# Token-half sums of a feed-forward layer kept in PSUM, with the norm ahead of the weights' sums

## The chip, the cores and the metric

The kernel runs on one core of a Trainium2 chip. The metric is the device time of one execution in microseconds (us). One core has a TensorE for matmuls (PE), with its weight loads shown apart (PEld), a VectorE (DVE), a ScalarE (ACT), a GpSimd (POOL), a SyncE whose queue starts the transfers (SP), and eight PSUM banks into which matmuls write.

## The reference, cut to what matters

A block of two layers works on 512 latent tokens and 256 context tokens, 1024 wide. The mixer of a layer is not touched. What is touched is the start of the feed-forward part:

```
def swiglu(h, w1, w3, w2):
    return (jax.nn.silu(h @ w1) * (h @ w3)) @ w2

x = x + ga_f * swiglu(rmsnorm(x, g_ffn[i]) * (1.0 + sc_f) + sh_f, w1[i], w3[i], w2[i])
ctx = ctx + cga_f * swiglu(rmsnorm(ctx, g_ffn[i]) * (1.0 + csc_f) + csh_f, w1[i], w3[i], w2[i])  # layer 0 only
```

`rmsnorm` divides each token by the root of its mean square. The inner width is 2816.

## The kernel before, in words

**The product in seven.** `h @ w1` and `h @ w3` are cut into jobs; a job is one of the two matrices, a part q and a chunk i. A job is computed as a 2x2 block product by a Winograd scheme of seven products in place of eight. Tokens are cut in two halves (layer 0: 384 and 384 columns, layer 1: 256 and 256), the 1024 inputs in two halves of four chunks of 128. b11 is the first half of the inputs for the first token half, b12 for the second, b21 and b22 the second half of the inputs. Product 1 needs b11 and product 2 needs b21. Products 7, 4, 5, 3 and 6 need sums, differences or copies of the four blocks: these are the operands, tiles `hp`, each held as a high and a low half (`hi` cast on ACT, `lo` the rest, on DVE or POOL). The weights of a product are sums of four blocks of the matrix in the same way (`wr` in, `S` and `wr` the sums, `wp` the two halves). Each product is 4 chunks by 3 matmuls (high by high, low by high, high by low; lines 398 to 400), 12 in all, into one PSUM bank (`f`). The program has eight of these banks and hands each bank out again when its last reader is done.

**The start of a layer's feed-forward.** `first_products` runs product 1 and then product 2 of the four lead jobs side by side. Then `run` goes on with the first two jobs alone, product by product, in the order 6, 7, 4, 5, 3 (`STEPS` without its first two), each for job 0 and then for job 1; the third job follows. While products 1 and 2 run, two chains of other work go on:

- `first_norm` makes the operands of products 1 and 2 from the first token half.
- `prepare` makes the rest. It is a generator: `first_products` takes a number of its steps after each chunk of products 1 and 2 (`PREP`), `run` one at every second product. It first takes the norm of the second token half: `rstd` is the reciprocal root, brought to all partitions by a matmul into a PSUM bank (line 619) after a reciprocal on DVE (line 615). `scaled` multiplies x by gain and `rstd` on DVE (line 1471, tile `hn`), `shifted` adds the bias on ACT (line 1479, tile `hf`). Four rounds then form, for each chunk, b12 - b11, T2 = b22 - that (operand of 6) and b21 - T2 (lines 1515, 1517, 1523 to 1525). Line 1528 makes the operand of 7, and `put` (lines 1461 and 1462) the two halves of the operands of 7, 4, 5 and 3 in that order.

**The weights.** `WeightStream.pump` runs ahead of the products. When the next task is one of a job's products it forms the sums that this product needs (`form`, lines 225 to 229, on DVE), casts the high half on ACT (line 183) and takes the low half on POOL or, for some products of `w1`, on DVE (line 188). It goes on until the weight tiles are used up, so the sums of the first two jobs stand in DVE's queue as soon as the tiles allow, whatever else waits behind them.

**What sets the order.** Every engine takes its instructions in the order in which the program was written out. An operation waits for the data and also for the last reader of the tile or PSUM bank that it overwrites.

**Results.** `complete` adds each product into the sums U (u[2], u[3]); `block` forms the gate (lines 1630, 1631) or the gated product (1634, 1635). Product 1's bank is copied out by ACT (line 1592).

Of the kernel before, what the change touches and what calls it, by code (L numbers as in the profile page):

```python
# [41 lines left out]
PREP = (0, 1, 1, 2), (1, 1, 1, 2)  # L42
# [4 lines left out]
STEPS = (1, 2, 6, 7, 4, 5, 3)  # L47
NCOL = 0.4219
# [10 lines left out]
class Job:  # L59
# [7 lines left out]
    def __init__(self, key, steps, time, pos=None):  # L67
        self.key, self.steps, self.time, self.pos = key, steps, time, pos
        self.units, self.raw, self.used, self.formed = None, {}, set(), set()
        self.u, self.home = {}, {}  # L70

# [30 lines left out]
class WeightStream:  # L102
# [6 lines left out]
    def __init__(self, kern, raws, parts):  # L109
# [7 lines left out]

        self.lead, self.dve = {}, {}
# [6 lines left out]

    def add_step(self, job, p, aps):
# [4 lines left out]
        if 1 in self.USES[p] and job.units[1] is None:  # L131
# [19 lines left out]
    def there(self, task):  # L151
# [4 lines left out]
        return all(i in what.raw or what.units[i] in self.raw for i in self.USES[p])  # L156
# [54 lines left out]
    def form(self, job, p):  # L211
# [5 lines left out]
        for i in self.USES[p]:  # L217
# [10 lines left out]
        if p == 7:  # L228
            v.tensor_sub(a12, a12, a11)  # L229
# [1134 lines left out]
class FeedForward:  # L1364
# [10 lines left out]
    def plan(self):  # L1375
# [59 lines left out]
    def begin(self, x, acc, streams, out):  # L1435
# [3 lines left out]
        self.h = [None] * NK  # L1439
        self.t = {}  # L1440
        self.prep = self.prepare()
        self.norm1 = Norm(self.first_norm())
# [21 lines left out]
    def scaled(self, rs, st, i):  # L1464

        k = self.k
        if self.h[i] is None:
            self.h[i] = k.act(name="hf")
        t = k.tmp(name="hn")
        for s, sl, at in pieces(st):  # L1470
            k.nc.vector.scalar_tensor_tensor(
                t[:, at], self.x[i][:, sl], k.gs[:, self.layer, 1, s, i : i + 1], rs[:, at], op0=OP.mult, op1=OP.mult
            )
        return t

    def shifted(self, t, st, i):
        k = self.k
        for s, sl, at in pieces(st):
            k.nc.scalar.activation(self.h[i][:, sl], t[:, at], AF.Identity, bias=k.mod[:, self.layer, 3, s, i : i + 1])

    def first_norm(self):
        st, n = self.streams[0], self.n
        nc = self.k.nc
        rs = yield from self.k.rstd(self.acc[st], st[1])
        yield 0
        for i in range(NK + 1):
            j = i - 1
            if i < NK:
                t = self.scaled(rs, st, i)
            if i > 0:  # L1490
                hi, lo = self.operand(1 + j // 4, j % 4)
                nc.scalar.copy(hi, self.h[j][:, :n])
            if i < NK:
                self.shifted(t, st, i)
            if i > 0:
                (nc.gpsimd if j % 2 else nc.vector).tensor_sub(lo, self.h[j][:, :n], hi.bitcast(F32))
                yield 0

    def prepare(self):

        st, n = self.streams[1], self.n
        nc = self.k.nc
        v = nc.vector
        rs = yield from self.k.rstd(self.acc[st], st[1], False)
        yield 0

        def block(e, i):
            return self.h[i + 4 * (e // 2)][:, n * (e % 2) : n * (e % 2) + n]
# [739 lines left out]
```

## Time and profile before

| | |
|---|---|
| three runs | 1699.99, 1701.46 and 1704.0 us, median 1701.46 |
| profiled execution | 1700.14 us, of which the span from the first to the last instruction is 1698.4 |
| mean granted clock of TensorE | 0.982 |
| busy: PE, PEld | 1601.1 us (94%), 1449.0 us (85%) |
| busy: DVE, POOL, ACT | 1178.8 us (69%), 818.6 us (48%), 741.9 us (44%) |

In the trace a row of an engine has its start, its duration, the line, the operation, the tile written and those read, and in brackets how long the engine stood idle ahead of it and which instruction ended that. Layer 0's feed-forward begins with product 1 at 448.0 us, layer 1's at 1307.6 us.

### The profile page before, as it was taken

How to read it: one execution, taken by the hardware profiler on the slowest of the kernel's cores; microseconds unless marked ns; L12 is line 12 of the kernel's file. 1: busy time of each engine (PE TensorE's matmuls, PEld its weight loads, DVE VectorE, ACT ScalarE, POOL GpSimd, SP SyncE). 2: the span in 40 equal slices, each digit the busy share in tenths (PEclk: the TensorE clock that was granted, in tenths of full speed). 3: DMA queues.
4: the chain of work that ended last, by engine and by line, in shares of the span. 5: the costliest groups of instructions: out<-in, count | busy, mean ns of one | idle time of the engine just before them, and what ended most of it. 6: DMA issues, size and time to landing. Idle time of an engine off the chain costs nothing. (4 is left out here: it accounts for less than half of the span.)

```text
span 1698.4 us, 26272 instructions
## 1 busy us (share of the span) xinstructions
PE 1601.1 (94%) x9730; PEld 1449.0 (85%) x9730; DVE 1178.8 (69%) x2054; ACT 741.9 (44%) x1437; POOL 818.6 (48%) x601
## 2 busy tenths in 40 slices
PE   6989999999979998999999999999999799999996
PEld 4867788888979987899999997779789789999996
DVE  6866566773777899586766776665666876766685
ACT  5534444653553223242332554444554544344343
POOL 3443232123375556465555623444125676666672
PEclk9999999999989999999999999999999899999998
DMA  9364253353023343434443345422232132332322
GB/s 355 139 199 138 67 160 97 119 170 130 26 76 111 103 134 120 129 125 137 149 137 118 127 161 163 135 73 74 80 131 81 60 115 75 111 114 76 94 87 69
DMA packets 76384, 202.28 MB, mean 119 GB/s; under 512 B 12704, under 2 KB 19488, under 8 KB 75872
## 3 DMA queue, kind: packets, MB, share of 16 engines
q1 hardware_dynamic: 76256, 200.60, 36.5%
q8 instruction: 77, 1.26, 0.3%
q14 instruction: 51, 0.42, 0.1%
HBM read 184.25 MB, written 11.80 MB: 115 GB/s over the span
## 5 line engine op out<-in xcount | busy, mean ns | idle before, releaser
L188 POOL TENSOR_TENSOR wp<-wr,wp 128x512 fp32r<-128x512 f32 (+1 forms) x336 | 465.7, 1399 | 311.0 <-ACT wp L183 306.2
L398 PE MATMUL f<-hp,wp 128*128 128x384 f32 (+1 forms) x1232 | 386.8, 314 | 14.8 <-DVE U L1599 4.2
L399 PE MATMUL f<-hp,wp 128*128 128x384 f32 (+1 forms) x1232 | 387.1, 314 | 10.8 <-DVE wp L188 6.2
L400 PE MATMUL f<-hp,wp 128*128 128x384 f32 (+1 forms) x1232 | 385.2, 313 | 4.0 <-POOL hp L1524 4.0
L183 ACT CAST wp<-wr 128x512 fp32r<-128x512 f32 (+1 forms) x360 | 213.3, 609 | 309.4 <-PE f L400 118.5
L188 POOL TENSOR_TENSOR wl<-wr,wh 128x1024 fp32r<-128x1024 f32 (+2 forms) x75 | 163.8, 2188 | 346.4 <-ACT wh L183 266.4
L398 PEld LDWEIGHTS f<-hp,wp 128*128 128x128 f32 x1232 | 238.0, 193 | 18.8 <-issue 8.2
L399 PEld LDWEIGHTS f<-hp,wp 128*128 128x128 f32 x1232 | 238.4, 193 | 15.3 <-POOL wp L188 8.5
L400 PEld LDWEIGHTS f<-hp,wp 128*128 128x128 f32 x1232 | 238.1, 193 | 5.1 <-POOL hp L1524 5.1
L398 PE MATMUL proj<-h,wh 128*128 128x512 f32 (+1 forms) x456 | 165.0, 362 | 1.0 <-DVE v L404 1.0
L398 PE MATMUL f<-g,wp 128*128 128x512 f32 (+1 forms) x468 | 160.5, 343 | 5.4 <-ACT g L1461 5.4
L400 PE MATMUL f<-g,wp 128*128 128x512 f32 (+1 forms) x468 | 160.5, 343 | 0.0
L399 PE MATMUL f<-g,wp 128*128 128x512 f32 (+1 forms) x468 | 160.3, 342 | 0.0
L399 PE MATMUL proj<-h,wl 128*128 128x512 f32 (+1 forms) x456 | 159.1, 349 | 0.7 <-POOL wl L188 0.7
L400 PE MATMUL proj<-h,wh 128*128 128x512 f32 (+1 forms) x456 | 158.9, 348 | 0.0
L1658 DVE SCALAR_TENSOR_TENSOR x<-f,mod,x 128x512 f32<-128x512 f32 (+1 forms) x130 | 79.0, 622 | 69.5 <-PE f L400 69.3
L398 PEld LDWEIGHTS proj<-h,wh 128*128 128x128 f32 x456 | 86.6, 190 | 25.5 <-issue 6.6
L522 DVE CUSTOM_DVE_ANT_0 adj<-wr,tab 128x1024 bf16<-128x1024 f32 x64 | 104.6, 1653 | 4.1 <-DMA wr<-in_w_adat_dram 4.0
L398 PEld LDWEIGHTS f<-g,wp 128*128 128x128 f32 x468 | 89.1, 190 | 17.0 <-ACT g L1461 6.8
L400 PEld LDWEIGHTS f<-g,wp 128*128 128x128 f32 x468 | 88.9, 190 | 11.2 <-DVE g L1462 1.1
L399 PEld LDWEIGHTS f<-g,wp 128*128 128x128 f32 x468 | 89.1, 190 | 9.9
L399 PEld LDWEIGHTS proj<-h,wl 128*128 128x128 f32 x456 | 86.8, 190 | 11.8 <-POOL wl L188 1.1
(251 smaller groups left out, 3415.2 us busy)
## 6 DMA issues: line engine op xcount, KB each, us to landing
wr<-in_w_dram SPq DMA_DIRECT2D x88, 512.0 KB
wr<-in_w_adat_dram SPq DMA_DIRECT2D x48, 512.0 KB
wr<-in_w_dram SPq DMA_DIRECT2D x80, 256.0 KB
wr<-in_w_ada_dram SPq DMA_DIRECT2D x32, 512.0 KB
ada<-in_w_ada_dram SPq DMA_DIRECT2D x16, 512.0 KB
wr<-in_w_out_dram SPq DMA_DIRECT2D x16, 512.0 KB
tab<-in_rpb_dram SPq DMA_DIRECT2D x12, 512.0 KB
strip<-strips SPq DMA_DIRECT2D x3, 1152.0 KB
```

The lines of the kernel that those rows point to most:

```text
L183: nc.scalar.copy(hi, src)
L188: (nc.vector if vector else nc.gpsimd).tensor_sub(lo, src, hi.bitcast(F32))
L398: mm(out, a[0], b[0], start=start, stop=False)
L399: mm(out, a[1], b[0], start=False, stop=False)
L400: mm(out, a[0], b[1], start=False, stop=stop)
L522: self.nc.vector.tensor_tensor_reduce(out=self.tmp(mybir.dt.bfloat16, D, "adj"), in0=raw, in1=self.tabs[("silu", s)], scale=1.0, scalar=0. ...
L1658: k.nc.vector.scalar_tensor_tensor(xs, ps[:, :n], k.mod[:, self.layer, 5, s, m : m + 1], xs, op0=OP.mult, op1=OP.add)
```

## The change

1. **The order of products** of the first two jobs goes from 6, 7, 4, 5, 3 to 3, 7, 6, 4, 5 (`FIRST`). Product 3 of these jobs needs the weights that were product 6's to form sums with (`uses`), u[2] and u[3] are both kept from product 1 (a second copy on ACT), and `complete` and `block` follow suit.
2. **The weights' sums wait** (`held`): `pump` stops ahead of the first job's product 3 until products 1 are written out, so that the norm of the second half comes ahead of them on DVE.
3. **`prepare` is written anew.** First it makes b22 for all four chunks and from it product 3's operand. Then, chunk by chunk, ACT writes b12 to a PSUM bank (a tile `T`, gain and bias in one step), DVE puts t3 = b22 - b12 in a second bank, and t1 = b12 - b11, the operand of 7 (from t3), t3 + b11 in b12's bank, the operand of 6 (from that) and b21 less it follow. Last come the operands of 5 and 4, chunk by chunk.

The number of matmuls and their shapes stay. DVE gets 12 instructions more (2044 to 2056 in the whole program), ACT 4 more, POOL 16 fewer.

```diff
-PREP = (0, 1, 1, 2), (1, 1, 1, 2)
+PREP = (0, 1, 1, 1), (1, 1, 1, 2)
+FIRST = (3, 7, 6, 4, 5)
...
+    def uses(self, job, p):
+        return (0, 1) if p == job.first else self.USES[p]
...
+        if 0 not in job.raw:
+            return
-        if p == 6:
+        if p == job.first:
             job.s1 = self.k.tmp(name="S1")[:, :n]
             v.tensor_add(job.s1, a21, a22)
             v.tensor_sub(a21, a11, a21)
             v.tensor_sub(a11, job.s1, a11)
-        if p == 7:
+        if p == (3 if job.first == 3 else 7):
             v.tensor_sub(a12, a12, a11)
...
     def pump(self):
             task = self.tasks[self.n_split]
+            if self.held and task[1] is self.held and task[0][1] == self.held.first:
+                self.issue()
+                break
...
-            j.steps = ()
-        self.order = [(j, p) for p in (1, 2) for j in lead] + [(j, p) for p in STEPS[2:] for j in two]
+            j.steps, j.first = (), FIRST[0]
+        self.order = [(j, p) for p in (1, 2) for j in lead] + [(j, p) for p in FIRST for j in two]
...
     def prepare(self):
-        for i in range(5):
-            if i < 4:
-                ts = [(j, self.scaled(rs, st, j)) for j in (i, i + 4)]
-            if i > 0:
-                b11, b12, b21, b22 = (block(e, i - 1) for e in range(4))
-                v.tensor_sub(b11, b12, b11)
-                t2 = self.k.tmp(name="T2")[:, :n]
-                v.tensor_sub(t2, b22, b11)
-            if i < 4:
-                for j, t in ts:
-                    self.shifted(t, st, j)
-            if i > 0:
-                hi, lo = self.operand(6, i - 1)
-                nc.scalar.copy(hi, t2)
-                nc.gpsimd.tensor_sub(lo, t2, hi.bitcast(F32))
-                nc.gpsimd.tensor_sub(b21, b21, t2)
-            yield 0
-        for i in range(4):
-            v.tensor_sub(block(1, i), block(3, i), block(1, i))
-        for p, e in ((7, 1), (4, 2), (5, 0), (3, 3)):
-            for i in range(4):
-                self.put(self.operand(p, i), block(e, i), i % 2)
+        for i in range(5):
+            if i < 4:
+                t = scaled(i + 4)
+            if i > 0:
+                hi, lo = self.operand(3, i - 1)
+                nc.scalar.copy(hi, late[i - 1][0])
+                gp.tensor_sub(lo, late[i - 1][0], hi.bitcast(F32))
...
+        ts = {0: scaled(0)}
+        for i in range(4):
+            b11, b21, (b22, t1) = self.h[i][:, :n], self.h[i][:, n : 2 * n], late[i]
+            b12, t3 = k.ps("T")[:, :n], k.ps("T")[:, :n]
+            shifted(b12, ts.pop(i), i)
+            v.tensor_sub(t3, b22, b12)
+            v.tensor_sub(t1, b12, b11)
+            (hi7, lo7), (hi6, lo6) = self.operand(7, i), self.operand(6, i)
+            nc.scalar.copy(hi7, t3)
+            v.tensor_sub(lo7, t3, hi7.bitcast(F32))
+            v.tensor_add(b12, t3, b11)
+            nc.scalar.copy(hi6, b12)
+            if i < 3:
+                ts[i + 1] = scaled(i + 1)
+            v.tensor_sub(lo6, b12, hi6.bitcast(F32))
+            v.tensor_sub(b21, b21, b12)
+            yield 0
+        for i in range(4):
+            self.put(self.operand(5, i), late[i][1], i % 2)
+            self.put(self.operand(4, i), self.h[i][:, n : 2 * n], 1 - i % 2)
+            if i % 2:
+                yield 0
...
     def first_products(self):
+            k.w.held = None
```

How the instructions stand before and now is shown at three places of layer 0; layer 1 has the same pattern. A number behind a name tells one tile from another. First DVE, from the end of the first token half's squares on, where product 1's last chunk runs. Before (`S` and `wr` are the weights' sums, `rs` the second half's reciprocal, `hn` what is scaled with it):

```order
L597 TENSOR_TENSOR sq_3901<-sq_3901,sq_4367 128x384 [waits DVE_49]
L225 TENSOR_TENSOR S_765_4422<-wr_4268 128x512 [waits DMAHW6_49]
L226 TENSOR_TENSOR wr_4268<-wr_3958,wr_4268 128x512 [waits DMAHW5_49,DVE_49,Pool_49]
L227 TENSOR_TENSOR wr_3958<-S_765_4422,wr_3958 128x512 [waits DVE_49,Pool_49]
L225 TENSOR_TENSOR S_767_4429<-wr_4320 128x512 [waits DMAHW7_49]
L226 TENSOR_TENSOR wr_4320<-wr_4027,wr_4320 128x512 [waits DMAHW2_49,DVE_49]
L227 TENSOR_TENSOR wr_4027<-S_767_4429,wr_4027 128x512 [waits DVE_49,Pool_49]
L615 RECIPROCAL rs_4463<-rs_4463 128x3 [waits Activation_49]
L1471 SCALAR_TENSOR_TENSOR hn_4488<-x_3876,gs,rstd_4251 128x384
```

The same place with the change:

```order
L611 TENSOR_TENSOR sq_3901<-sq_3901,sq_4366 128x384 [waits DVE_49]
L629 RECIPROCAL rs_4449<-rs_4449 128x3 [waits Activation_49]
L1495 SCALAR_TENSOR_TENSOR hn_4473<-x_3876,gs,rstd_4251 128x384
L1504 TENSOR_TENSOR hp_4475<-hf_4308,hp_4475 128x384 [waits Activation_49]
L1520 TENSOR_TENSOR hn_4494<-x_3870,rstd_4448 128x384 [waits PE_49]
L1520 TENSOR_TENSOR hn_4499<-x_3872,rstd_4448 128x384
L1520 TENSOR_TENSOR hn_4507<-x_3874,rstd_4448 128x384 [waits DVE_49]
L236 TENSOR_TENSOR S_786_4527<-wr_4268 128x512 [waits DMAHW6_49]
L237 TENSOR_TENSOR wr_4268<-wr_3958,wr_4268 128x512 [waits DMAHW5_49,DVE_49,Pool_49]
L238 TENSOR_TENSOR wr_3958<-S_786_4527,wr_3958 128x512 [waits DVE_49,Pool_49]
L240 TENSOR_TENSOR wr_3958<-wr_3958 128x512 [waits DVE_49,Pool_49]
```

The reciprocal and the first three `hn` of the second half have moved ahead of the weights' sums, and the sums now stand between the third `hn` and the fourth, eight in a row for the two jobs (line 236 opens each four).

The second place is DVE further on, where the last two chunks' sums are made. Before:

```order
L1515 TENSOR_TENSOR hf_4308<-hf_4308 128x384
L1517 TENSOR_TENSOR T_800_4600<-hf_4407,hf_4308 128x384 [waits DVE_49,Activation_49]
L1515 TENSOR_TENSOR hf_4350<-hf_4350 128x384 [waits Activation_49]
L1517 TENSOR_TENSOR T_802_4623<-hf_4487,hf_4350 128x384 [waits DVE_49,Activation_49,Pool_49]
L1528 TENSOR_TENSOR hf_4297<-hf_4357,hf_4297 128x384
```

The third chunk's turn and the start of the fourth with the change (`T` are the tiles in PSUM, `rstd_4448` the second half's reciprocal root, in PSUM too):

```order
L1553 TENSOR_TENSOR T_4643<-hf_4512,T_4642 128x384 [waits DVE_49,Activation_49]
L1554 TENSOR_TENSOR hf_4512<-T_4642,hf_4308 128x384
L1557 TENSOR_TENSOR hp_4648<-T_4643,hp_4648 128x384 [waits Activation_49]
L1558 TENSOR_TENSOR T_4642<-T_4643,hf_4308 128x384 [waits DVE_49]
L1520 TENSOR_TENSOR hn_4654<-x_3868,rstd_4448 128x384
L1562 TENSOR_TENSOR hp_4649<-T_4642,hp_4649 128x384 [waits Activation_49]
L1563 TENSOR_TENSOR hf_4308<-hf_4308,T_4642 128x384
L1553 TENSOR_TENSOR T_4659<-hf_4566,T_4658 128x384 [waits DVE_49,Activation_49]
```

A chunk's turn has seven DVE operations now, six of which read or write a `T` tile, and the last reader of `rstd_4448` (`hn_4654`) stands in the third chunk's turn, 30 DVE instructions behind the third `hn` of the place above.

The third place is PE, where products 2 end and the first two jobs go on alone. Before, with product 6 of job 0:

```order
L400 MATMUL f_4551<-hp_4494,wp_4419 128x384
L398 MATMUL f_4687<-hp_4532,wp_4426 128x384 [waits Activation_49]
L399 MATMUL f_4687<-hp_4532,wp_4426 128x384
L400 MATMUL f_4687<-hp_4532,wp_4426 128x384 [waits Pool_49]
L398 MATMUL f_4687<-hp_4577,wp_4426 128x384 [waits Activation_49]
```

With the change, product 3 of job 0:

```order
L414 MATMUL f_4548<-hp_4479,wp_4416 128x384
L412 MATMUL f_4693<-hp_4501,wp_4532 128x384 [waits DVE_49,PE_49,Activation_49]
L413 MATMUL f_4693<-hp_4501,wp_4532 128x384 [waits Pool_49]
L414 MATMUL f_4693<-hp_4501,wp_4532 128x384
L412 MATMUL f_4693<-hp_4509,wp_4532 128x384
```

The first matmul behind products 2 waited for ACT alone, and now also for DVE. The bank of `f_4693` is the one that `rstd_4448` held, and the DVE instruction that it waits for is the one that writes `hn_4654`. Product 3 of job 1 and products 7 of both jobs take the banks of the `T` tiles in the same way, of the third chunk and of the fourth. Behind the loop, ACT's queue has the operands of 5 and 4 in turn, each waiting for the low half of the one just ahead of it; before it had those of 7, 4, 5 and 3, of which those of 5 waited for the low half of the one two ahead and those of 3 for the one just ahead.

## Rows read from the trace of the kernel before

**Rows 1.** The profile page, busy time of each engine.

```profile
PE 1601.1 (94%) x9730; PEld 1449.0 (85%) x9730; DVE 1178.8 (69%) x2054; ACT 741.9 (44%) x1437; POOL 818.6 (48%) x601
```

**Rows 2.** Timeline of PE, layer 0: start, us, line, operation, tiles, idle before.

```profile
456.75 0.51 PE L619 MATMUL rstd<-cst,rs 128*128 128x128 f32 x3 [1.01 <-DVE rs L615]
...
462.29 0.44 PE L398 MATMUL f<-hp,wp 128*128 128x384 f32 x1 [1.37 <-ACT gate L1592]
...
469.16 0.33 PE L398 MATMUL f<-hp,wp 128*128 128x384 f32 x1
...
473.87 0.59 PE L400 MATMUL f<-hp,wp 128*128 128x384 f32 x1 [1.75 <-POOL hp L1524]
474.26 0.52 PE L398 MATMUL f<-hp,wp 128*128 128x384 f32 x1
474.58 0.52 PE L399 MATMUL f<-hp,wp 128*128 128x384 f32 x1
...
482.35 0.69 PE L399 MATMUL f<-hp,wp 128*128 128x384 f32 x1 [3.58 <-DVE wp L188]
...
501.62 0.41 PE L398 MATMUL f<-hp,wp 128*128 128x384 f32 x1 [2.15 <-DVE U L1599]
```

**Rows 3.** Windows by engine: stretch, its us, busy time, then PE's clock.

```profile
480.00:485.00 5.00, 2.65 (x8) 2.65 (x9) 5.00 (x4) 0.37 (x1) 5.00 (x4) 0.58 0.00 0
```

**Rows 4.** Timeline of PE, layer 1.

```profile
1316.83 0.47 PE L619 MATMUL rstd<-cst,rs 128*128 128x128 f32 x2 [3.86 <-DVE rs L615]
...
1325.78 0.28 PE L398 MATMUL f<-hp,wp 128*128 128x256 f32 x1
...
1335.64 0.58 PE L399 MATMUL f<-hp,wp 128*128 128x256 f32 x1 [2.59 <-DVE wp L188]
...
1354.04 0.41 PE L398 MATMUL f<-hp,wp 128*128 128x256 f32 x1
```

**Rows 5.** Timeline of DVE, layer 0, the weights' sums and the reciprocal behind them.

```profile
452.01 0.69 DVE L226 TENSOR_TENSOR wr<-wr,wr 128x512 f32<-128x512 f32 x1
...
454.93 1.59 DVE L227 TENSOR_TENSOR wr<-S,wr 128x512 f32<-128x512 f32 x1
456.45 0.16 DVE L615 RECIPROCAL rs<-rs 128x3 f32<-128x3 f32 x1
```

**Rows 6.** Timeline of ACT, layer 0: root, a cast behind DVE, the weights' casts.

```profile
454.12 0.26 ACT L614 ACTIVATE rs<-ssq,eps 128x3 f32<-128x3 f32 x1
...
470.45 0.51 ACT L1523 CAST hp<-T 128x384 fp32r<-128x384 f32 x1 [0.64 <-DVE T L1517]
...
477.67 2.18 ACT L183 CAST wp<-wr 128x512 fp32r<-128x512 f32 x4
...
486.33 1.28 ACT L1631 ACT_TABLE_LOAD   x1
```

**Rows 7.** Timeline of POOL, layer 0.

```profile
454.29 1.68 POOL L188 TENSOR_TENSOR wp<-wr,wp 128x512 fp32r<-128x512 f32 x1 [2.91 <-ACT wp L183]
...
490.68 1.02 POOL L1462 TENSOR_TENSOR hp<-hf,hp 128x384 fp32r<-128x384 f32 x1 [0.62 <-ACT hp L1461]
...
497.77 1.02 POOL L1462 TENSOR_TENSOR hp<-hf,hp 128x384 fp32r<-128x384 f32 x1 [1.76 <-ACT hp L1461]
```

**Rows 8.** Timeline of DVE, layer 0, sums of token halves, splits, a gate.

```profile
475.44 5.20 DVE L1462 TENSOR_TENSOR hp<-hf,hp 128x384 fp32r<-128x384 f32 x4
480.56 1.74 DVE L188 TENSOR_TENSOR wp<-wr,wp 128x512 fp32r<-128x512 f32 x1
...
490.98 0.57 DVE L1635 TENSOR_TENSOR f<-f,gate 128x384 f32<-128x384 f32 x1
```

**Rows 9.** Layer 1: DVE's step, then the tail on ACT and POOL (three timelines).

```profile
1318.98 0.41 DVE L1515 TENSOR_TENSOR hf<-hf 128x256 f32<-128x256 f32 x1
...
1331.99 2.17 ACT L183 CAST wp<-wr 128x512 fp32r<-128x512 f32 x4
...
1346.09 1.81 POOL L1462 TENSOR_TENSOR hp<-hf,hp 128x256 fp32r<-128x256 f32 x2
```

More of the change, by code (lines that the diff above doesn't have):

```diff
@@ L130, in add_step @@
             self.units.append(aps[0])
-        if 1 in self.USES[p] and job.units[1] is None:
+        if 1 in self.uses(job, p) and job.units[1] is None:
             job.units[1] = len(self.units)
@@ L155, in there @@
         p = key[1]
-        return all(i in what.raw or what.units[i] in self.raw for i in self.USES[p])
+        return all(i in what.raw or what.units[i] in self.raw for i in self.uses(what, p))
     def need(self, task):
@@ L1462, in put, with block @@
         (nc.gpsimd if pool else nc.vector).tensor_sub(lo, src, hi.bitcast(F32))
[L1464 to L1479, printed above, removed]
     def first_norm(self):
         st, n = self.streams[0], self.n
-        nc = self.k.nc
-        rs = yield from self.k.rstd(self.acc[st], st[1])
+        k, nc = self.k, self.k.nc
+        rs = yield from k.rstd(self.acc[st], st[1])
         yield 0
+        ((s, sl, _),) = pieces(st)
+        def block(j):
+            return self.h[j % 4][:, n * (j // 4) : n * (j // 4) + n]
         for i in range(NK + 1):
@@ L1510, in prepare, with shifted @@
+        def shifted(out, t, i):
+            for s, _, at in pieces(st):
+                nc.scalar.activation(
+                    out[:, at], t[:, at], AF.Identity,
+                    bias=k.mod[:, self.layer, 3, s, i : i + 1], scale=k.gs[:, self.layer, 1, s, i : i + 1],
+                )
         for i in range(5):
             if i < 4:
-                ts = [(j, self.scaled(rs, st, j)) for j in (i, i + 4)]
+                t = scaled(i + 4)
             if i > 0:
-                b11, b12, b21, b22 = (block(e, i - 1) for e in range(4))
@@ new lines, in prepare @@
+                late[i] = both[:, :n], both[:, n : 2 * n]
+                del both
+                shifted(late[i][0], t, i + 4)
+            if i == 2:
+                yield 0
+        del t
+        yield 0
[15 more added lines that the diff above has]
+            v.tensor_sub(b21, b21, b12)
+            del b22, t1, t3, b12
@@ L1547, in product @@
         del w
-        if p == 6 and self.homes and job is self.order[1][0]:
+        if p == FIRST[0] and self.homes and job is self.order[1][0]:
             self.homes.clear()
@@ L1574, in first_products @@
                 for j in jobs[:2]:
-                    j.home[6] = j.home[1]
-            for j, b in zip(jobs, ps):
+                    j.home[FIRST[0]] = j.home[1]
+            for j in jobs:
+                b = ps.pop(0)
                 if p == 1:
@@ L1590, in complete @@
         if p == 1:
-            u[2] = self.place(job, 0)
-            self.k.nc.scalar.copy(u[2], ps)
+            for r in (0, 1) if job.first == 3 else (0,):
+                u[2 + r] = self.place(job, r)
+                self.k.nc.scalar.copy(u[2 + r], ps)
         elif p == 2:
@@ L1596, in complete @@
             add(u[2], u[2], ps)
+            if 3 in u:
+                add(u[3], u[3], ps)
         elif p == 7:
-            u[3] = self.place(job, 1)
-            add(u[3], u[2], ps)
+            if job.first == 3:
+                add(u[3], u[3], ps)
+            else:
+                u[3] = self.place(job, 1)
+                add(u[3], u[2], ps)
         elif p == 4:
@@ L1604, in complete @@
             self.block(job, 1, 1, ps, u.pop(3))
+            if job.first == 3:
+                self.block(job, 0, 1, ps, u.pop(2), True)
+        elif job.first == 3:
+            add(u[2], u[2], ps)
         else:
@@ L1620, in gate, with block @@
         return self.gates[key]
-    def block(self, job, r, c, ps, u):
+    def block(self, job, r, c, ps, u, done=False):
         k, n = self.k, self.n
@@ L1629, in block @@
         if x == "w1":
-            nc.vector.tensor_add(gate, ps, u)
+            if not done:
+                nc.vector.tensor_add(gate, ps, u)
             nc.scalar.activation(gate, gate, AF.Silu)
             return
-        nc.vector.tensor_add(ps, ps, u)
-        nc.vector.tensor_mul(ps, ps, gate)
+        if not done:
+            nc.vector.tensor_add(ps, ps, u)
+            u = ps
+        nc.vector.tensor_mul(ps, u, gate)
         if c == 1:
```

44 lines of the change are left out of this document (27 added, 17 removed).

## The prediction

> **What bounds the kernel now.** The page's first part comes first: PE is busy for 94% of the span [rows 1], so whatever keeps it from a matmul at full clock is on the path. Next comes PE's timeline in the two places where a layer's feed-forward begins. In layer 0, PE stands 1.01 us ahead of the matmul that spreads `rstd`, 1.37 for a bank of product 2 that ACT has still to copy, 1.75 inside product 6 for an operand that POOL makes, 3.58 inside product 7 for DVE's half of the weights, and 2.15 ahead of the last product of the two jobs [rows 2]. Behind the longer waits matmuls last 0.52 at a pitch of 0.32 [rows 2], where 0.33 at 0.17 is usual, and the granted clock from 480 to 485 is 0.58 [rows 3], near the lower of the two levels: a pause costs again after it ends. The first matmul of the two jobs alone is at 469.16; the third job begins at 503.7, twelve matmuls behind 501.62 [rows 2]. Between them 120 matmuls at 0.173 are 20.8 us, so 13.8 are lost. Layer 1 has the same picture, with 3.86 for `rstd` and 2.59 in product 7 [rows 4].
>
> DVE's timeline says why. The root that `rstd` needs is done on ACT at 454.38 [rows 6], but the reciprocal runs at 456.45, behind the weights' sums [rows 5]. From there DVE is full until product 7's weights at 480.56 [rows 8]. So DVE sets this place, and the question is what it must now do ahead of PE's next matmul.
>
> **The change, part by part, layer 0.**
>
> *The norm ahead of the sums.* The reciprocal can run at about 454.4, and `rstd`'s matmul at 456.75 - 1.01 = 455.7 without a wait: 1.0 won. The wait for the bank shrinks too, since ACT has three shifts to make there and not eight; I take 0.6 of its 1.37. PE then ends products 2 at 469.16 - 1.6 = 467.6.
>
> *What now stands ahead of PE's next matmul.* By the order, the first matmul of product 3 waits for the third turn's `hn` on DVE, because its bank is `rstd`'s. Before, product 6 took a bank that only ACT's copy had to free. So I add up DVE's queue:
> - Three `hn` from 456.1, at a pitch of about 0.5: 457.6.
> - Eight sums of weights. From the one at 452.01 to the one at 454.93 are four steps, 0.73 each, and beside a POOL split one takes 1.59 [rows 5, 7], 0.9 more. Eight steps are 5.8, and I count three such meetings, 2.7: 466.1. Without a meeting, 463.4.
> - ACT's cast of product 3's weights (0.55) with a hand-over on either side, and DVE's half of them, 1.74 [rows 8]: 469.0. Two more `hn`: 470.0. ACT puts b12 into PSUM, two pieces: the first turn begins at 471.5. With no meetings at all and DVE's half at 0.7 (between 0.69 and 1.74), 468.
> - A turn is a chain: t3, cast, low half, sum, cast, low half. A DVE step that waits for the one ahead takes 0.57 to 0.6 [rows 8], a cast 0.51 [rows 6], and b21's step comes at the end: 4 x 0.6 + 2 x 0.51 + 0.2 = 3.6. Below it cannot go under seven steps at 0.46, 3.2. Above, seven at the 1.30 that DVE's splits take beside POOL [rows 8] would be 9.1; POOL has little to do in these turns, and the `T` operands lie in PSUM, so I take 3.6.
> - The third turn's `hn` ends at 471.5 + 2 x 3.6 + 2.6 = 481.3.
>
> The trace has one row for the last point: DVE's step on an `f` in PSUM at 490.98 took 0.57 though POOL's split began at 490.68 [rows 7, 8], while DVE's splits from SBUF at 475.44 took 1.30 each [rows 8]. The Trainium skill, "SBUF — State Buffer", section "Who interferes with whom", says that a DVE instruction with two SBUF inputs contends with a POOL instruction that reads SBUF and one with at most one SBUF input does not; the rows agree. By that rule the turns are safe, but the same rule speaks against the other half of the change: all eight weights' sums have two SBUF inputs and still lie in a stretch with POOL's splits. With it the sums end at 466.1, without it at 463.4.
>
> PE thus stands from 467.6 to 481.3, 13.7 us. This is the largest term of all. It takes the place of product 6's and 7's own waits.
>
> *Products 3, 7 and 6* of both jobs: 72 matmuls at 0.173 are 12.5. Behind the pause some 16 run at 0.32, as behind product 7's [rows 2], 2 more: 495.8. Their banks and operands are there by then (the turns end at about 484.9), so nothing else is on the path.
>
> *The operands of 5 and 4.* Product 4 is now fourth, and its last operand is the last that is made. Before, the last made was product 3's, which came fifth; it was ready at 497.77 + 1.02 = 498.8 [rows 7], 21.1 behind the weights' casts at 477.67 [rows 6]. Now: five weight casts behind the turns, the fifth behind three POOL splits, 4.9; the table load 1.28 [rows 6] and the gate 0.5: 491.6. Then eight operands one behind another, since each cast waits for the low half ahead: four at 0.51 + 0.57 + 0.1, four on POOL at 0.51 + 1.02 + 0.1, 11.3, and the gated product's cast between them, 1.6: 504.5. That is 19.6 behind the turns' end, a little under the 21.1 of before. PE has product 4 of job 0 but for its last chunk long before, and stands some 8 us. Then 36 matmuls, 6.2, and 1.5 to 2 at the half clock: the third job begins at 512.5, against 503.7: **+8.8**. Bounds: +5.5 (no meetings), +11 (half clock throughout).
>
> **Layer 1.** `rstd`'s 3.86 goes [rows 4], and about 0.6 of half clock behind it: PE is ready at 1325.78 - 4.5 = 1321.3. The sums stood ahead of the root in part; now they begin behind three `hn` at 1314 and take 8.5: 1322.5. Cast, half, two `hn` and shift, 4.7: 1327.2. A step is 0.41 [rows 9] where it was 0.55, a turn 2.8: the third `hn` ends at 1334.8, and PE stands 13.5. Six products are 72 x 0.12 = 8.6 and 2.3 of half clock: 1345.7. The tail: turns end at 1337.5; 4.9 and the gate, then eight operands at 0.41 + 0.43 or 0.41 + 0.74 to 0.92 [rows 9] with 0.1, 8.8 to 9.5, and 1.2: about 1352.5. Before it was 1331.99 to 1347.9, 15.9 [rows 9]; now 15. Product 4's rest and three products, 4.3, bring the third job to about 1356.5, where before it began at 1354.0 [rows 4]: **+2.5**, between -1 and +5. So layer 1 gives back what its entry wins.
>
> The other edits (a second ACT copy for two jobs, 12 more DVE instructions) lie in these chains or beside PE, and I cost them at nothing; the copies' cover is PE's product 2, and without it they are 0.4 each.
>
> **Sum.** +8.8 + 2.5 = +11.3 against the profiled execution's 1700.14, which is 1.3 under the median of 1701.46. The same difference on the median is 1712.8; I say 1712.
>
> **Rivals.**
>
> *Faster: the tail is hidden.* Product 4's operands would be there when PE has done products 3, 7 and 6. Then PE's pause of 13.7 about equals the 13.8 lost in before, and the entry's gains stay: -1.6 in layer 0. In layer 1 the lost time of before is about the new pause with its half clock, and 4.5 stays: -4.5. Together -6: 1695. For it speaks that the operands are fewer than before by eight. Against it speaks the count: it needs the tail in 11 us and not 19.6. 0.12.
>
> *No change: both chains at their lower bounds.* The turns begin at 468 and take 3.2, and the tail is 2 us shorter: layer 0 +3, layer 1 -3, so 1701. For it: every step has a row that short. Against: three long stretches would all have to run undisturbed, and in before POOL was busy beside most of DVE's work. 0.18.
>
> *Slower than forecast: the clock falls twice.* PE pauses for 13.7 and then for 8 in each layer. If each pause is followed by more than 16 matmuls at 0.32, say 36, and the chunks of product 4 that wait one by one for operands run at it as well, that is 20 x 0.147 + 2 more in layer 0 and the like in layer 1, +8: 1720. 0.10. It decides if the clock stays low between two short bursts.
>
> *The change does not do what it says* would be a reciprocal still behind the sums. The order rules that out: it stands ahead of all eight.
>
> The forecast keeps 0.60. The range: the bounds of the two layers, +4.5 and +16, and the middle of the no-change case lie inside 1700 to 1720; most of the faster case and part of the slower lie outside, about 0.2. A measurement of this kernel can tell about 0.2%, 3.4 us, from no change. Slower by more: forecast and the slower rival, 0.70. Within: 0.18. Faster: 0.12.
>
> **What would show it.** In the profile of the changed kernel: PE's first matmul of product 3 with 13 us of idle time ended by DVE's `hn` of line 1520, in both layers; no wait of PE for the reciprocal (line 629); eight sums in a row on DVE at 0.7 to 1.6 between the third and the fourth `hn`; turns of 3.6 and 2.8; a second pause of PE, in product 4 of job 0, ended by an operand's low half (line 1477); the third job at about 512.5 and 1356.5, each less by what stands ahead of it. I am wrong if product 3 starts within 5 us of product 2's end, or if the pause in product 4 is short: then the serial chain behind the turns is where the sum fails. I am also wrong if a stretch far from these two places moves by over 2 us, since every other stage should only shift.

## The result: 0.7% slower

The changed kernel takes 1716.84 us (median of four runs, 1710.57 to 1718.36) where the kernel before takes 1702.73 in the same comparison: a ratio of 1.0071, with a 95% interval of 1.0051 to 1.0091 (the ratio is estimated over all the runs; the two medians by themselves are 14.1 us apart). One execution of run 1 below ran at a mean granted clock of 0.437 and took 3646.37 us; it is left out of that run's time and ratio. The profiled execution took 1718.36 us, its span 1716.6, 18.2 more than the span of before.

Not all of these 18.2 us belong to the change. The two programs issue 9730 matmuls of the same shapes in the same sequence (products change places, their sizes do not), so the n-th of one can be set against the n-th of the other, its counterpart. The first matmul of product 1 in layer 0 starts at 453.03 us and in before at 448.00: 5.0 us later, though nothing ahead of it was touched. The experiments below have the same program up to there, and in their profiles it starts anywhere from 448.9 to 453.2; run 7, which is the kernel before in all of layer 0, has 453.16. That is spread between executions. Most of the 5.0 us, 4.3, is there by the 200th matmul, at 44.6 us; the windows of before and then of the changed kernel (stretch, its us, busy time of PE, PEld, DVE, ACT and POOL, then PE's granted clock, the transfers' busy share and GB/s) show the granted clock at 1.00 and at 0.88 there, though whether that is the cause is not shown:

```profile
20.00:48.00 28.00, 24.17 (x198) 18.41 (x198) 24.41 (x51) 15.98 (x29) 11.06 (x8) 1.00 0.95 351
```

```profile
20.00:48.00 28.00, 25.37 (x180) 18.65 (x181) 20.37 (x42) 14.27 (x25) 10.53 (x8) 0.88 0.90 337
```

I count from the start of product 1 in each layer from here on. The table gives the start of a matmul in the changed kernel less that of its counterpart in before, in us, each counted from the start of product 1 in its layer.

| | layer 0 | layer 1 |
|---|---|---|
| first matmul of product 2 | -1.2 | -5.2 |
| first matmul of the two jobs alone | +12.2 | +8.1 |
| 72 matmuls on (product 4 of job 0) | +6.9 | +2.5 |
| third job | +10.9 | +1.2 |
| 72 matmuls into it | +9.4 | +2.6 |

The last line makes +12.0 over the two layers, and the ratio makes 12.1 of 1702.7, with an interval of 8.7 to 15.5. Product 3 starts late, some of that comes back within 72 matmuls (5.3 us in layer 0, 5.6 in layer 1), and in layer 0 4.0 is lost again in products 4 and 5.

The profile page of the changed kernel, busy time of each engine: PE's share went from 94% [rows 1] to 93%, with the same matmuls.

```profile
PE 1603.3 (93%) x9730; PEld 1449.6 (84%) x9730; DVE 1166.8 (68%) x2066; ACT 746.7 (44%) x1441; POOL 801.1 (47%) x585
```

The timeline of PE in the changed kernel, layer 0 and then layer 1, answers [rows 2, 4]:

```profile
460.61 0.49 PE L633 MATMUL rstd<-cst,rs 128*128 128x128 f32 x3
...
466.38 0.44 PE L412 MATMUL f<-hp,wp 128*128 128x384 f32 x1 [1.62 <-ACT gate L1631]
...
486.35 0.66 PE L412 MATMUL f<-hp,wp 128*128 128x384 f32 x1 [12.92 <-ACT hp L1559]
...
505.01 0.45 PE L412 MATMUL f<-hp,wp 128*128 128x384 f32 x1 [3.46 <-DVE g L1477]
...
510.49 0.69 PE L412 MATMUL f<-hp,wp 128*128 128x384 f32 x1 [1.47 <-ACT hp L1476]
...
1348.45 0.55 PE L412 MATMUL f<-hp,wp 128*128 128x256 f32 x1 [12.16 <-ACT hp L1559]
```

The wait for `rstd` is gone. In its place stand 12.92 us ahead of product 3 in layer 0 and 12.16 in layer 1. The row names ACT's cast of line 1559, which ended last by the profile. By the program the matmul waits for DVE's `hn` of the third turn, and the times fit that: in the rows below `hn` ends at 485.66 + 0.55 = 486.21, and PE starts 0.14 later; in layer 1 the two are 0.15 apart.

The timeline of DVE in the changed kernel, layer 0, answers [rows 5, 8]:

```profile
458.91 0.18 DVE L629 RECIPROCAL rs<-rs 128x3 f32<-128x3 f32 x1 [3.70 <-ACT rs L628]
...
461.14 1.48 DVE L1520 TENSOR_TENSOR hn<-x,rstd 128x384 f32<-128x384 f32 x3 [1.08 <-PE rstd L633]
...
463.31 0.69 DVE L237 TENSOR_TENSOR wr<-wr,wr 128x512 f32<-128x512 f32 x1
464.11 1.32 DVE L238 TENSOR_TENSOR wr<-S,wr 128x512 f32<-128x512 f32 x1
465.53 1.30 DVE L240 TENSOR_TENSOR wr<-wr 128x512 f32<-128x512 f32 x1
...
468.99 1.59 DVE L240 TENSOR_TENSOR wr<-wr 128x512 f32<-128x512 f32 x1
...
476.17 0.56 DVE L1553 TENSOR_TENSOR T<-hf,T 128x384 f32<-128x384 f32 x1 [2.10 <-ACT T L1525]
...
479.89 0.56 DVE L1553 TENSOR_TENSOR T<-hf,T 128x384 f32<-128x384 f32 x1
...
485.66 0.55 DVE L1520 TENSOR_TENSOR hn<-x,rstd 128x384 f32<-128x384 f32 x1
...
510.47 0.56 DVE L1477 TENSOR_TENSOR hp<-hf,hp 128x384 fp32r<-128x384 f32 x1 [3.81 <-ACT hp L1476]
```

DVE stands idle for 3.70 us until the root is there, makes three `hn` and then the eight sums until 470.58, and begins the turns at 476.17, one every 3.72 us. The last row is the low half of the last operand of product 4.

The windows of the changed kernel, read as the two above, answer [rows 3]:

```profile
486.00:491.00 5.00, 4.65 (x15) 4.68 (x16) 4.17 (x9) 3.19 (x8) 0.35 (x1) 0.50 0.01 2
505.00:510.00 5.00, 3.69 (x9) 2.27 (x9) 1.66 (x3) 1.40 (x4) 3.23 (x3) 0.54 0.01 5
510.00:515.00 5.00, 4.51 (x14) 4.42 (x15) 4.46 (x6) 1.83 (x4) 1.91 (x2) 0.50 0.00 0
```

Behind the pause ahead of product 3 the granted clock is 0.50 of full speed, the lower of the two levels. From product 4's start it is 0.54 and then 0.50, until 515.

### The profile page after: what moved, and what is told of

Same layout as the page of the kernel before. It is cut to its first block, busy times and chain, and to the rows that moved or that the text cites. A ratio compares the mean times of both kernels' runs of the same rounds, so it can differ in the third digit from the quotient of the medians.

```text
span 1716.6 us, 26278 instructions
## 1 busy us (share of the span) xinstructions
PE 1603.3 (93%) x9730; PEld 1449.6 (84%) x9730; DVE 1166.8 (68%) x2066; ACT 746.7 (44%) x1441; POOL 801.1 (47%) x585
```

## Experiments

Two accounts were open. By the **chain account**, DVE's turns and then the operands of 5 and 4, made one behind another, set the start of the third job, and where PE pauses before that matters little. By the **bank account**, the pause ahead of product 3 is the loss, and taking the bank away gives it back. A third question was what the norm's early place is worth by itself. The table has all runs with the numbers of the table above: the two jobs alone (A), 72 matmuls on (B), the third job (C) and 72 matmuls into it (D), each less its counterpart in before.

| | ratio (95%) | layer 0: A, B, C, D | layer 1: A, B, C, D |
|---|---|---|---|
| changed kernel | 1.0071 (1.0051 to 1.0091) | +12.2, +6.9, +10.9, +9.4 | +8.1, +2.5, +1.2, +2.6 |
| 1 sums in SBUF | 1.0061 (1.0046 to 1.0077) | -0.9, +6.1, +9.4, +8.0 | -4.3, +1.2, -0.1, +1.8 |
| 2 lows on DVE | 1.0053 (1.0039 to 1.0067) | +12.2, +6.1, +8.4, +7.0 | +8.1, +2.5, +3.6, +2.4 |
| 3 before, norm first | 1.0003 (0.9994 to 1.0013) | -1.4, +2.2, +4.0, +2.7 | -4.5, -0.5, -1.7, -0.5 |
| 4 sums ahead of the norm | 1.0080 (1.0065 to 1.0096) | +10.1, +5.7, +9.2, +7.7 | +7.8, +2.8, +1.5, +3.0 |
| 5 four before five | 1.0055 (1.0038 to 1.0072) | +12.1, +5.3, +5.7, +6.0 | +8.1, +2.5, +1.2, +2.6 |
| 6 three together | 1.0041 (1.0025 to 1.0057) | -0.9, +5.1, +5.4, +5.6 | -4.3, +1.3, -0.2, +1.3 |
| 7 before, norm first in layer 1 | 1.0000 (0.9989 to 1.0011) | -0.2, -0.5, -0.2, -0.2 | -4.5, -0.5, -1.7, -0.3 |
| 8 longer turns | one run | +15.2, +10.9, +14.3, +12.9 | +10.2, +5.3, +5.7, +5.4 |

### 1. The sums in SBUF

```diff
-            b12, t3 = k.ps("T")[:, :n], k.ps("T")[:, :n]
+            b12, t3 = k.tmp(name="T")[:, :n], k.tmp(name="T")[:, :n]
```

> The changed kernel, with both tiles of a chunk's turn (b12 and t3) in SBUF in place of two PSUM banks, so that no bank stands between product 2 and product 3. Chain theory (DVE's turns and then the one-by-one operands of 5 and 4 set the start of the third job, whatever PE does in between): product 3 starts within 3 us of product 2's end, the pause moves into product 7, product 4 of job 0 still ends with its last operand, and the time is that of the changed kernel less 0 to 3 us, 1712 to 1717. Bank theory (the 13 us for the bank of rstd are the loss): most of the two pauses comes back, 10 us or more, 1707 or less.

It took 1714.88 us, its ratio 1.0 part in a thousand under the changed kernel's. The two intervals overlap, so the ratios alone do not tell the two apart; the stretches do, by 1.4 us in layer 0 and 0.8 in layer 1 (D). The timeline of PE in layer 0:

```profile
470.28 0.33 PE L412 MATMUL f<-hp,wp 128*128 128x384 f32 x1
...
478.05 0.45 PE L412 MATMUL f<-hp,wp 128*128 128x384 f32 x1 [1.65 <-ACT hp L1556]
...
485.53 0.69 PE L412 MATMUL f<-hp,wp 128*128 128x384 f32 x1 [2.41 <-ACT hp L1556]
...
489.38 0.69 PE L413 MATMUL f<-hp,wp 128*128 128x384 f32 x1 [0.98 <-POOL wp L197]
...
501.19 0.69 PE L412 MATMUL f<-hp,wp 128*128 128x384 f32 x1 [3.60 <-DVE g L1477]
506.67 0.69 PE L412 MATMUL f<-hp,wp 128*128 128x384 f32 x1 [1.47 <-ACT hp L1476]
```

The bank was what product 3 waited for: with the `T` tiles out of the banks it starts 13 us earlier, at once behind product 2 (the first row). But the pause is only cut in pieces. Product 7 now waits for the operand of each turn (1.65 and 2.41 in the rows, 2.71 between them), then for the weights behind the turns, and product 4 begins 0.8 us earlier than in the changed kernel and the third job 1.4. The chain account holds; the bank account, which asked for 10 us or more, falls.

### 2. The low halves on DVE

```diff
-            self.put(self.operand(5, i), late[i][1], i % 2)
-            self.put(self.operand(4, i), self.h[i][:, n : 2 * n], 1 - i % 2)
+            self.put(self.operand(5, i), late[i][1], False)
+            self.put(self.operand(4, i), self.h[i][:, n : 2 * n], False)
```

> The changed kernel, with the low halves of the operands of 5 and 4 all on DVE (0.56 us each there, 1.02 on POOL; four of eight move in each layer). Chain theory: in layer 0, where the casts wait one by one, the last operand comes 4 x 0.45 = 1.8 us earlier and so does the third job; in layer 1 the casts ran together and little changes: 1714 to 1716 where the changed kernel has 1716.8, that is 1 to 3 us less. Bank theory: the pause ahead of product 3 is untouched, so no change, within 1 us.

It took 1712.92 us, a little below the expected range; here too the interval of the ratio overlaps the changed kernel's. In layer 0 the third job came 2.5 us earlier than in the changed kernel, in layer 1 it came 2.4 later, and 72 matmuls on 0.2 earlier. The timeline of ACT in layer 0 shows the step of the tail, one cast behind one low half; the wait of 0.62 covers DVE's 0.56:

```profile
496.99 0.51 ACT L1476 CAST hp<-hf 128x384 fp32r<-128x384 f32 x1 [0.62 <-DVE hp L1477]
498.20 0.51 ACT L1476 CAST hp<-hf 128x384 fp32r<-128x384 f32 x1 [0.70 <-DVE hp L1477]
499.34 0.51 ACT L1476 CAST hp<-hf 128x384 fp32r<-128x384 f32 x1 [0.62 <-DVE hp L1477]
```

In the changed kernel two of these three steps wait for POOL:

```profile
498.40 0.52 ACT L1476 CAST hp<-hf 128x384 fp32r<-128x384 f32 x1 [0.62 <-DVE hp L1477]
500.05 0.51 ACT L1476 CAST hp<-hf 128x384 fp32r<-128x384 f32 x1 [1.13 <-POOL hp L1477]
501.68 0.51 ACT L1476 CAST hp<-hf 128x384 fp32r<-128x384 f32 x1 [1.12 <-POOL hp L1477]
```

A step is 1.14 to 1.21 us with DVE and 1.63 to 1.65 with POOL. Four such steps make 1.8 us, and the third job of layer 0 came 2.5 earlier: the tail is on the path in layer 0.

### 3. The norm first, in the kernel before

```diff
             task = self.tasks[self.n_split]
+            if self.held and task[1] is self.held and task[0][1] == 6:
+                self.issue()
+                break
 ...
         self.prep = self.prepare()
+        k.w.held = self.order[0][0]
 ...
+            k.w.held = None
             ws = w = None
```

> The kernel before with one part of the change alone: the weights' sums of the first job wait until products 1 are written out, so the second half's norm comes ahead of them on DVE. If PE's wait for rstd is what the part wins (1.0 in layer 0, 3.9 with its half clock in layer 1): 4 to 6 us faster than before. If DVE is the path there and the part only leaves it idle until the root is there (from 450.2 to 454.4 in layer 0, from 1310 to 1313 in layer 1), the operands and weights behind come later by that and the wait moves to products 6 and 7: 3 to 7 us slower than before.

1703.93 us, a ratio of 1.0003: neither number. The table says why: the two accounts share the layers, and each holds in part. In layer 0 product 6 starts 1.4 us earlier, but the third job comes 4.0 later; in layer 1 product 6 starts 4.5 earlier, the third job 1.7, and 72 matmuls on 0.5 is left. The timeline of DVE in layer 0 of this kernel has the price:

```profile
449.75 1.32 DVE L601 TENSOR_TENSOR sq<-sq,sq 128x384 f32<-128x384 f32 x1
454.78 0.18 DVE L619 RECIPROCAL rs<-rs 128x3 f32<-128x3 f32 x1 [3.71 <-ACT rs L618]
...
457.00 2.69 DVE L1476 SCALAR_TENSOR_TENSOR hn<-x,gs,rstd 128x128 f32<-128x128 f32 x8 [1.08 <-PE rstd L623]
```

DVE is idle for 3.71 us, and 1.08 more, where before it was at the weights' sums. The whole queue behind it comes that much later.

### 4. The sums ahead of the norm, in the changed kernel

```diff
-        k.w.held = self.order[0][0]
```

> The changed kernel without that part: the weights' sums go ahead of the norm as in the kernel before; the rest of the change stays. If the norm's early place is a gain: PE waits for rstd again, 3 to 5 us in each layer, and the kernel is 4 to 9 us slower than the changed one. If DVE's queue sets the start of product 3: the turns begin some 5 us earlier in each layer, because DVE no longer stands idle for the root, product 3 and the third job follow, and the kernel is 6 to 10 us faster than the changed one, 1707 to 1711.

1717.43 us, a ratio of 1.0080 where the changed kernel has 1.0071: again neither. `rstd` waits again, and product 3 starts only 2.1 us earlier in layer 0 and 0.3 in layer 1. The timelines in layer 0, of PE and then, in the next two fences, of ACT and DVE:

```profile
462.39 0.51 PE L633 MATMUL rstd<-cst,rs 128*128 128x128 f32 x3 [2.36 <-DVE rs L629]
...
483.50 0.66 PE L412 MATMUL f<-hp,wp 128*128 128x384 f32 x1 [7.97 <-DVE hn L1519]
```

```profile
462.78 0.62 ACT L1501 ACTIVATE hf<-hn,mod 128x384 f32<-128x384 f32 x1 [3.15 <-DVE hn L1494]
...
467.61 0.83 ACT L1630 COPY gate<-f 128x384 f32<-128x384 f32 x2
...
472.23 1.06 ACT L1524 ACTIVATE T<-hn,mod,gs 128x128 f32<-128x128 f32 x2
```

```profile
466.30 0.56 DVE L1519 TENSOR_TENSOR hn<-x,rstd 128x384 f32<-128x384 f32 x1 [0.88 <-ACT hf L1524]
473.32 0.56 DVE L1552 TENSOR_TENSOR T<-hf,T 128x384 f32<-128x384 f32 x1 [6.46 <-ACT T L1524]
```

DVE is ready for the first turn at 466.9, and then waits 6.46 us for ACT. ACT waits until 462.78 for an `hn`, which DVE makes behind the sums and the reciprocal, and from there it works without a pause until the first `T` is written: shifts, casts, the copies of product 1's banks and a cast of weights stand ahead of it in the queue. So DVE's queue was not the only thing ahead of the turns: with DVE's share moved away, ACT's queue is late next. The first turn begins 2.1 us earlier than in the changed kernel, counted from product 1, where I had expected 5. What the norm's early place is worth cannot be told from nothing in either kernel. This run also names DVE's `hn` as what ends product 3's wait, as the program has it.

### 5. The operands of 4 before those of 5

```diff
         for i in range(4):
-            self.put(self.operand(5, i), late[i][1], i % 2)
-            self.put(self.operand(4, i), self.h[i][:, n : 2 * n], 1 - i % 2)
-            self.h[i] = late[i] = b11 = b21 = None
-            if i % 2:
-                yield 0
+            self.put(self.operand(4, i), self.h[i][:, n : 2 * n], i % 2)
+            self.h[i] = None
+        yield 0
+        for i in range(4):
+            self.put(self.operand(5, i), late[i][1], i % 2)
+            late[i] = None
+        yield 0
```

> The changed kernel with the last eight operands in another order: all four of product 4, then all four of product 5, where they were made in turn chunk by chunk. Nothing else moves and product 4 is still fourth. If the one-by-one tail behind the turns sets the third job: product 4 of job 0 has its operands by its start and the last operand is needed 24 matmuls later than before, so the third job begins 5 to 6 us earlier in layer 0 and 2 to 3 us earlier in layer 1: 1707 to 1711 where the changed kernel has 1716.8. If the pause ahead of product 3 is what costs: no change, within 1.5 us.

1712.1 us, 1.1 above the expected range. Layer 0 did what the chain account says: the third job comes 5.2 us earlier than in the changed kernel, with product 4's start still waiting. Of the 5.2 us 3.4 are left 72 matmuls on: a wait of 0.65 us, 60 matmuls into the third job, has grown to 2.45 (the last row). Layer 1 did not move at all, where 2 to 3 us had been expected; why is said in the next section. The timeline of PE in layer 0 of this kernel; the first two rows are the only waits of over 2 us between product 2 and the third job:

```profile
483.02 0.66 PE L412 MATMUL f<-hp,wp 128*128 128x384 f32 x1 [12.90 <-ACT hp L1559]
...
500.06 0.69 PE L412 MATMUL f<-hp,wp 128*128 128x384 f32 x1 [2.99 <-DVE g L1477]
...
524.20 0.44 PE L412 MATMUL f<-hp,wp 128*128 128x384 f32 x1 [2.45 <-DVE g L1477]
```

The second wait of product 4 of the changed kernel, 1.47 at 510.49, is gone. The first stays: product 4 of job 0 takes the bank of a product 2, whose last reader is DVE's low half of the gated product, and that stands in the queues behind four of the operands.

### 6. The three together

This is run 5 with all eight low halves on DVE, as in run 2, and the `T` tiles in SBUF, as in run 1.

> The order of the run before (operands of 4, then of 5), with the low halves of these eight on DVE and with the tiles of the turns in SBUF, so that no bank holds up products 3. If the three costs add up (6 to 9 us, 2 to 4 us and 0 to 3 us): 1703 to 1707, about the kernel before. If the turns on DVE and ACT alone are a floor that the tail hides behind: no better than the run before, 1708 to 1710.

1708.75 us, a ratio of 1.0041: the lowest of the changed kernel's versions, but not the kernel before. The three gains are 1.0, 1.8 and 1.6 parts in a thousand by themselves, 4.4 in sum, and 3.0 together. With intervals of 1.4 to 2.0 parts to either side that neither shows nor rules out that they add up. The timeline of PE in layer 0, two of its eight waits between products 2 and the third job:

```profile
486.02 0.69 PE L412 MATMUL f<-hp,wp 128*128 128x384 f32 x1 [2.46 <-ACT hp L1556]
...
500.75 0.69 PE L412 MATMUL f<-hp,wp 128*128 128x384 f32 x1 [3.20 <-DVE g L1477]
```

Product 4 still begins 5.1 us later than in before, for the gated product behind the turns. In layer 0 that is where the rest of the loss, 5.6 us, stands. How much of it is the length of the turns, and how much the weights' casts that wait behind them, was not tried.

### 7. The norm first, in layer 1 alone

This is run 3 with one more condition:

```diff
-        k.w.held = self.order[0][0]
+        k.w.held = self.order[0][0] if self.last else None
```

> The kernel before, with the norm ahead of the weights' sums in layer 1 only, where the run with both layers won about 1.9 us between the start of product 1 and the end, while it lost 2.7 in layer 0. If these two numbers are real and belong to this part: 1 to 3 us faster than before, 1701 to 1703 where before has 1704.0, which is at the limit of what can be told. If they are spread between two profiles: no change.

The median is 1703.46 us against 1702.52, and the ratio over all the runs 1.0000: it can't be told from before. In the profile layer 1's third job begins 1.7 us earlier than in before, the same as in run 3, and the end of the kernel comes 2.0 earlier, counted from layer 1's product 1. The ratio's interval reaches 1.9 us to either side. So no version here is shown to be faster than the kernel before.

### 8. Longer turns

```diff
             v.tensor_sub(t1, b12, b11)
+            v.tensor_sub(t1, b12, b11)
+            v.tensor_sub(t1, b12, b11)
```

> The changed kernel with b12 - b11 formed three times in every turn in place of once: two DVE steps more in each, about 0.9 us in layer 0 and 0.65 in layer 1. If DVE's turns are on the path through the bank to product 3 and through the tail to the third job: product 3 starts 2.5 to 2.8 us later in layer 0 and 1.8 to 2.0 later in layer 1, and the third job 3.2 to 3.8 and 2.3 to 2.6 later, each counted from the start of product 1. If PE waits for ACT's weights' casts, or for operands from POOL, instead: neither moves by over 1 us.

It took 1720.15 us, in one execution. Product 3 starts 3.0 us later than in the changed kernel in layer 0 and 2.1 in layer 1, a little more than expected. The third job comes 3.5 later in layer 0, as expected, and 4.5 in layer 1, well over the 2.3 to 2.6 (2.8 by 72 matmuls on). The timeline of PE:

```profile
487.46 0.66 PE L412 MATMUL f<-hp,wp 128*128 128x384 f32 x1 [15.93 <-ACT hp L1561]
```

A turn is 4.72 us here, 1.00 longer, and what is added to the turns is added to the pause and to the third job. The turns are on the path.

## Why the prediction was right

The prediction was 1712, between 1700 and 1720, with 0.70 on slower. The mechanism held: DVE's queue and the bank set product 3, and the turns and the operands behind them set the third job of layer 0. The sum, +11.3 forecast and +12.1 measured, is nearer than its two terms were: the third job came 2.1 us later than forecast in layer 0 and 1.3 earlier in layer 1, and that these misses nearly cancel is luck. By the prediction's own steps, layer 0 in times less the 5.03 us by which this execution was late:

- *The entry.* `rstd`'s matmul ran without a wait at 455.6 (predicted 455.7). PE ended products 2 at 468.2, not 467.6: the wait for the bank of product 2 did not shrink, it grew from 1.37 to 1.62. ACT has fewer shifts there, but it now makes two copies of one bank for each of the first two jobs, a cost that the prediction had put at nothing.
- *DVE's queue.* The sums ended at 465.6 (466.1), with three of eight drawn out to 1.30 to 1.59, as counted. By the Trainium skill, "SBUF — State Buffer", section "Who interferes with whom", a DVE instruction with two SBUF inputs contends with a POOL instruction that reads SBUF. The trace agrees: the three long sums stand beside POOL's splits (the rows below), and of the prediction's two values, 466.1 and 463.4, the one with the long sums was right. A sum that began just ahead of a POOL split, at 463.31 in the rows of DVE, kept 0.69. The turns began at 471.1 (471.5), a turn took 3.72 (3.6), the third `hn` ended at 481.2 (481.3), and product 3 started at 481.3 (481.3). The step on which most rested was right to a tenth, and run 1 showed that the bank is what it waits for. The timeline of POOL in the changed kernel, layer 0:

```profile
463.34 2.94 POOL L1537 TENSOR_TENSOR hp<-hf,hp 128x384 fp32r<-128x384 f32 x2 [1.47 <-ACT hp L1536]
468.45 1.58 POOL L197 TENSOR_TENSOR wp<-wr,wp 128x512 fp32r<-128x512 f32 x1 [2.17 <-ACT wp L192]
```

- *Products 3, 7 and 6* ended at 496.4 (495.8).
- *The tail* ended at 506.0 (504.5), the last operand 1.5 us late: 0.7 of it passed ahead of the first cast and 0.8 in the eight operands and the gated product. This is the larger part of layer 0's miss. Run 2 and run 5 showed that the tail sets the third job in layer 0.
- *Product 4 of job 0* went otherwise than forecast. "PE has product 4 of job 0 but for its last chunk long before" was wrong: its first matmul waited 3.46 us for the bank of a product 2, until 500.0, and the last chunk 1.47 more for its operand. A short pause in product 4 was one of the prediction's signs of being wrong, and it came half true: 4.9 us in two pieces here, and 3.4 in layer 1, where some 8 were forecast. The first wait did not set the third job, since the last operand was later. Behind that operand 15 matmuls ran at the lower clock, until 515.4 - 5.0 = 510.4, some 2.4 us longer than at the higher, where the forecast held 1.5 to 2. The third job came at 514.7 (512.5): the term is +10.9 and not +8.8, 1.5 of the difference from the tail and the rest from behind it.
- *Layer 1.* Product 3 started 8.1 us later than product 6 in before; the prediction's times make it 1334.8 against 1325.8, +9.0. The third job was at +1.2 (+2.5). Less the 14.6 us by which product 1 of layer 1 was late, the tail's last operand was there at 1350.3 (1352.5), 2.2 us early; some 0.9 of it went again behind it. About 1 us of the 2.2 is the turns, which began earlier: the eight sums took 7.6 us and not 8.5. The other is the tail, and there the mechanism was wrong. The prediction carries layer 0's rule over, each cast behind the low half of the one ahead, and counts 8.8 to 9.5 us for the eight operands and 1.2 for the gated product. In layer 1 ACT's casts run four at a stretch, as they do in the kernel before, and all of it took 6.6 us from the first cast on (1358.26 to 1364.86). The waits shown for ACT's queue, each operand's cast behind a low half, are thus those of layer 0 alone; why layer 1 does without them stays open. In the other direction, the 1.28 us of a table load at 1356.64 are not in the prediction's sum for layer 1. Product 4 waited 2.97 us for its bank, but for a low half of the tail only 0.41, and run 5, which changes the tail's order, moved nothing here.
  The timeline of PE, layer 1, product 4 of job 0:

```profile
1361.82 0.39 PE L412 MATMUL f<-hp,wp 128*128 128x256 f32 x1 [2.97 <-DVE g L1477]
...
1364.04 0.58 PE L414 MATMUL f<-hp,wp 128*128 128x256 f32 x1 [0.41 <-POOL hp L1477]
```

  The timeline of ACT, layer 1, in the changed kernel and then in before:

```profile
1358.26 1.31 ACT L1476 CAST hp<-hf 128x256 fp32r<-128x256 f32 x4
...
1361.66 1.32 ACT L1476 CAST hp<-hf 128x256 fp32r<-128x256 f32 x4
```

```profile
1344.66 1.32 ACT L1461 CAST hp<-hf 128x256 fp32r<-128x256 f32 x4
```

- *The rivals.* "The tail is hidden" did not occur. "The clock falls twice" did in the granted clock: PE ran at 0.50 of full clock behind both pauses of layer 0, and at 0.50 again from 1362.5 to 1365 in layer 1. Its price did not come about: in layer 0 the lower clock behind the last operand cost some 2.4 us, of which the forecast held 1.5 to 2, and not the rival's 8 in all.
- *What I had named as a gain* was none. The sum took the entry as 1.6 and 4.5 us won. Runs 3 and 4 show that the win is spent on the way: DVE, idle until the root is there, begins its queue later, and with the old order ACT is late next. In layer 1 alone (run 7) 1.7 us are left at the third job, which the run's time can't tell from nothing.
- *Not taken apart.* No run has the new order of products, or the second copies on ACT, by itself. With all three remedies (run 6) 1.0041 is left, and of that nothing is shown but that the turns are on the path (run 8).

A stretch far from the two places should not have moved by over 2 us. The first 448 us moved by 5.0, with the same program, and run 7 has as much. Between 72 matmuls into the third job of layer 0 and product 1 of layer 1 the difference moved by 0.2 us here, and by up to 2.6 in the experiments (run 1), where the same matmuls run on the same operands; I take it for spread as in the first 450 us, but that is not shown.

The bank account's remainder: the pauses of product 3 were the largest rows of the profile, and removing them was worth about 2 us (run 1: 1.7 by the ratio, with overlapping intervals, and 2.2 by the stretches). What set the time in layer 0 was what was made last, not the longest wait.

## What to carry to other kernels

A pause of the busiest engine is worth what is left of it when the work behind has been walked through to the end; taking away two pauses of 13 and 12 us here gave about 2, because the same operands and weights were late next. Where temporaries are kept in PSUM banks, ask which matmul gets each bank afterwards and behind which instruction in another engine's queue the bank's last reader stands. And make operands in the order in which the products use them: here that alone brought the third job 5.2 us earlier (3.4 by 72 matmuls on) in the layer whose tail was serial, and nothing in the other. A chain read in one layer need not be that of the next: look for its waits in each.

## What the runs showed of the hardware

- For these turns PSUM and SBUF cost the same. With the tiles in SBUF (run 6) the steps with two SBUF inputs took 0.55 to 0.56 us, a turn 3.74; with them in PSUM 0.55 to 0.56 and 3.72. POOL was idle beside them for over 14 us in both (14.44 and 14.40), so these runs say nothing of turns beside a busy POOL. The timeline of DVE and of POOL in run 6:

```profile
488.13 0.55 DVE L1563 TENSOR_TENSOR hf<-hf,T 128x384 f32<-128x384 f32 x1
```

```profile
488.22 5.84 POOL L197 TENSOR_TENSOR wp<-wr,wp 128x512 fp32r<-128x512 f32 x4 [14.44 <-ACT wp L192]
```

- The same instructions ahead of the change reached product 1 of layer 0 between 448.0 and 453.2 us in ten profiles. A single profile therefore says little about 0.2% of the whole, while the difference inside a stretch, counted from its own start, repeated to some tenths: -4.5 and -1.7 in layer 1 of runs 3 and 7 alike.
